# Weights stationary, tokens moving: turning the first product of two feed-forwards round, from the third chunk on

## The chip, the core and the metric

The kernel runs on one core of a Trainium2 chip, as one program in one launch. The engines named here are TensorE (matrix products and transposes, "PE"; its weight loads are a row of their own, "PEld"), VectorE ("DVE"), ScalarE ("ACT"), GpSimd ("POOL") and SyncE ("SP", which issues most DMAs). On-chip memory is SBUF for operands and PSUM for the results of TensorE. The metric is the device time of one execution in microseconds (us), and lower is better. Three runs of the kernel before gave a median of 793.23 us, from 792.94 to 793.36.

## The reference, cut to what matters

One layer of a residual block on 256 tokens of width 1024: a feed-forward, a mixer of two branches, a cross-attention on a memory, and a second feed-forward. Everything is in float32. Only the two feed-forwards are touched; both are this:

```
x = x + 0.5 * rmsnorm(swiglu(rmsnorm(x, pre_g), w_in, w_down), post_g)
def rmsnorm(x, g):  return x * rsqrt(mean(x*x) + 1e-6) * g
def swiglu(h, w_in, w_down):
    gate, up = split(h @ w_in, 2)          # w_in 1024 x 5632
    return (silu(gate) * up) @ w_down      # w_down 2816 x 1024
```

The per-token factor of the first rmsnorm can be taken out of the product: h @ w_in is that factor times (x * pre_g) @ w_in. So the kernel multiplies the unnormalised x and applies the factor, called r2 (one number per token, for each half of 128 tokens), to the results.

## The kernel before

**Split operands.** A float32 number is held as two parts, hi (rounded by a copy to the matmul type) and lo (what is left). A product of two such numbers is made of three: hi with hi, hi with lo, lo with hi, added up in PSUM. Each weight unit is 128 rows by 1024 columns (512 KB): `load_split` loads it as `raw` (4 buffers), ScalarE casts `hi` (line 142) and VectorE subtracts `lo` (line 144). `hi` and `lo` have 8 buffers each, used in turn; a new unit can be cast only when the unit eight places earlier is no longer read by TensorE. A unit of `w_in` holds two blocks of 128 contracted rows by 512 columns, so a chunk of the feed-forward has four units; a chunk of `w_down` has two.

**The feed-forward** (`ffn`, line 352) goes over 11 chunks of 256 hidden columns (`NFF` = 11). A chunk's first product gives 256 gate and 256 up columns, 512 in all. In the token form (`proj_tok`, line 184) the 128 tokens of one half are stationary and the 512 weight columns move: 8 contraction blocks by 3 products for each half, so 48 matmuls of 512 columns for a chunk. `act_evac` (line 370) takes a half's result out of PSUM: ScalarE applies silu to the gate with the scale r2, VectorE multiplies up by r2 and by that. The result has tokens on the partitions; the second product needs hidden columns there, so `flush` (line 358) makes four transposes on TensorE, and `split` (line 161) copies hi and subtracts lo from the transposed tile. `down` (line 401) is the second product of a chunk: 24 matmuls of 512 columns for both halves, into four PSUM banks that stay open over all chunks.

**Order.** After the first product of chunk c comes the second product of chunk c-2, with the transposes of chunk c placed 21 matmuls into it (`L_ACT`). Chunks 8 to 10 (`STAG` = 3) are left for a tail, first half of the tokens first, with `post` or, at the very end of the kernel, `post_last` for the second rmsnorm and the addition to x. In the first feed-forward chunks 0 to 2 are done in a form that goes over the contraction outermost, both halves at once (`act_first`), because the weights are still arriving. In the second, chunks 0 and 1 are done for one half of the tokens while the other half of x is not ready.

**Who orders the rest.** The program's order gives priorities; a planner places each engine's instructions by its own estimates, and `after(i)` ties instructions to the i-th matmul of a running log. Each engine then works in its own fixed order, so an instruction that waits holds all behind it on that engine.

**PSUM.** Eight banks: four `acc`, two `mm`, two `tr` (function `trp`).

**The row of factors.** Where tokens lie along the free dimension, a factor per token must be a row on all partitions. `row_of` (line 270) makes it for other stages: VectorE transposes a small tile that holds the factors (line 273), GpSimd's queue writes it to DRAM (line 275) and reads it back to all partitions (line 277).

`proj_col` (line 193) is a form used elsewhere in the kernel in which the weights stand and 256 tokens move, three matmuls of 256 columns per contraction block.

Of the kernel before, what the change touches and what calls it, by code (L numbers as in the profile page):

```python
# [36 lines left out]
L_LAST = 8  # L37
# [42 lines left out]
def block_kernel(ctx: ExitStack, tc: tile.TileContext, wts, head_in, gf_in, x_in, mem_in, memT_in, cols, rows, fbias, masks, out):  # L80
# [102 lines left out]

    def proj_tok(ps, X, units, h, n=512):
# [64 lines left out]
    def ssq(dst, src):  # L249
        S.activation(junk[:, : src.shape[-1]], src, AF.Square, accum_out=dst)  # L250
# [9 lines left out]
    fac = [cp.tile([P, 64], F32, name=nm("fac")) for _ in range(2)]  # L260
# [49 lines left out]
    def post(ps, h, grow, factor=1.0, store=False):  # L310

        s = s1(2, name="ss2")
        ts = []
        for j in range(2):
            ssq(s[:, j : j + 1], ps[j])
            t = sp.tile([P, 512], F32, tag="z2", name=nm("post"), bufs=3)
            V.scalar_tensor_tensor(out=t, in0=ps[j], scalar=-factor * SC_RSTD, in1=grow[:, j * 512 : (j + 1) * 512], op0=ALU.mult, op1=ALU.mult)
            ts.append(t)
# [6 lines left out]
    def post_last(ps, h, grow, factor):  # L325

        s = s1(2, name="ss2")
        ts = []
        for j in range(2):
            ssq(s[:, j : j + 1], ps[j])  # L330
# [9 lines left out]
            V.scalar_tensor_tensor(out=t, in0=ps[j], scalar=-factor * 16.0, in1=grow[:, j * 512 : (j + 1) * 512], op0=ALU.mult, op1=ALU.mult)  # L340
# [11 lines left out]
    def ffn(w_in, w_dn, X, r2, n_tok, i_row, first_half, second_half=None):  # L352

# [16 lines left out]
        def act_evac(ps, c, h):  # L370
            sg = sp.tile([P, FC], F32, tag="c1", name=nm("sg"), bufs=7)
            silu = S.activation(sg, ps[:, :FC], AF.Silu, scale=r2[h])  # L372
            if c == NFF - 1 and h == 1 and not first_half:
                with tc.issue_after(silu.ins):
                    S.activation(warm, ones[:, 0:1], AF.Abs_reciprocal_sqrt)
            a = sp.tile([P, FC], F32, tag="c1", name=nm("at"), bufs=7)
            V.scalar_tensor_tensor(out=a, in0=ps[:, FC:], scalar=r2[h], in1=sg, op0=ALU.mult, op1=ALU.mult)  # L377
# [4 lines left out]
        def act_tok(c, h):  # L382
            ps = mm()
            proj_tok(ps, X, chunk(w_in, c), h)
            act_evac(ps, c, h)

# [26 lines left out]
        for h in range(2):  # L413
# [3 lines left out]
            if h == 0 and n_tok:  # L417
                second_half(m)
        accs = None
        done = 0  # L420
        if callable(r2):
            outs = act_first((0, 1), acc)
            r2 = r2()
            for c in range(2):
# [4 lines left out]
        for c in range(n_tok, NFF):  # L429
# [7 lines left out]
            else:  # L437
                for h in range(2):
                    n = len(log)
                    act_tok(c, h)  # L440
                    if c == 2 or c > NFF - STAG + 1 and h == 0:
                        flush(n + L_ACT)
# [7 lines left out]
            while done < min(c - 1, NFF - STAG):  # L450
# [795 lines left out]
```

## Time and profile before

| what | value |
|---|---|
| median of 3 runs | 793.23 us (792.94 to 793.36) |
| profiled execution, its own time | 791.78 us |
| its span, first to last instruction | 790.0 us |
| clock granted to TensorE | 0.998 of full speed |
| PE busy / weight loads busy | 99% / 86% |
| VectorE / ScalarE / GpSimd busy | 66% / 54% / 2% |
| one chunk in the steady part of a feed-forward | 16.80 us |

Busy shares are over the whole span. In the chain that ended last, each piece is the work, or the wait, that the next one waited for, so its shares say where the time is. A TensorE row's mean duration is that of one matmul from its start to its modelled end; since matmuls overlap, what a matmul costs in a row of them is the distance between starts.

### The profile page before, as it was taken

To read this page: it belongs to the slowest core of one execution; us is meant where nothing else is said; L and a number is where in the kernel's file an instruction comes from. 1 tells how busy PE (TensorE), PEld (TensorE's weight loads), DVE (VectorE), ACT (ScalarE), POOL (GpSimd) and SP (SyncE) were. 2 spreads that over 40 slices of the span, in tenths; PEclk is the share of its full clock that TensorE was granted. 3 is DMA by queue.
4 is the path that set the end of the run, shared out by engine and by line. 5 is a ranking of instruction groups with operands and counts; after the bars stand their busy time and mean duration, and the time that the engine had idled before them with its cause. 6 is when DMAs were issued, how large, how long until landed. Compare 5 with 4: busy or idle time off the path is not lost.

```text
span 790.0 us, 12203 instructions
## 1 busy us (share of the span) xinstructions
PE 782.3 (99%) x4736; PEld 677.4 (86%) x4736; DVE 519.0 (66%) x825; ACT 426.8 (54%) x656; POOL 13.7 (2%) x36
## 2 busy tenths in 40 slices
PE   9999999999999999999999999999999999999996
PEld 7888888888899999998788888999888888888885
DVE  6774545557767899488686666964669754545543
ACT  7654444546664677357774345643657644434541
POOL 0000000000000102100000000000000000000000
PEclk9999999999999999999999999999999999999999
DMA  9786654563654547634576654555263655554521
GB/s 347 247 271 205 228 189 160 188 202 118 210 196 144 180 136 224 258 120 152 197 251 222 211 191 160 164 186 181 65 229 134 227 199 209 203 200 161 183 84 54
DMA packets 44345, 147.82 MB, mean 187 GB/s; under 512 B 5048, under 2 KB 8768, under 8 KB 44288
## 3 DMA queue, kind: packets, MB, share of 16 engines
q1 hardware_dynamic: 43168, 144.83, 53.9%
q0 software_dynamic: 688, 1.85, 1.0%
q8 instruction: 37, 0.61, 0.3%
q10 hardware_dynamic: 432, 0.37, 0.1%
q14 instruction: 20, 0.16, 0.1%
HBM read 145.97 MB, written 1.06 MB: 186 GB/s over the span
## 4 chain that ended last, share of the span: by engine, by line
PE 98%; DMA 1%; DVE 0%; ACT 0%; SPq 0%; issue 0%; DVEq 0%; ACTq 0%
PE mm L94 68%; PE acc L94 27%; PE tr L367 1%; PE tr L94 1%; PE tr L294 1%; DMA head<-in_head_dram 1%; PE tr L898 0%; PE tr L989 0%; PE acc L1099 0%; DVE xs L348 0%; DVE post L340 0%; ACT hi L507 0%; SPq L491 0%; ACT hT L285 0%; SPq L486 0%
## 5 line engine op out<-in xcount | busy, mean ns | idle before, releaser
L144 DVE TENSOR_TENSOR lo<-raw,hi 128x1024 fp32r<-128x1024 f32 (+1 forms) x256 | 306.7, 1206 | 122.4 <-ACT hi L142 114.3
L142 ACT CAST hi<-raw 128x1024 fp32r<-128x1024 f32 (+1 forms) x256 | 262.4, 1038 | 149.3 <-PE mm L94 83.3
L94 PE MATMUL mm<-lo,hT 128*128 128x512 f32 (+1 forms) x592 | 226.9, 385 | 0.0
L94 PE MATMUL mm<-hi,hT 128*128 128x512 f32 (+1 forms) x592 | 226.8, 385 | 0.0
L94 PE MATMUL mm<-hi,lT 128*128 128x512 f32 (+1 forms) x592 | 226.5, 385 | 0.0
L94 PEld LDWEIGHTS mm<-hi,lT 128*128 128x128 f32 x592 | 111.2, 188 | 21.4 <-DVE lT L286 0.2
L94 PEld LDWEIGHTS mm<-hi,hT 128*128 128x128 f32 x592 | 111.2, 188 | 21.4 <-ACT hT L285 0.3
L94 PEld LDWEIGHTS mm<-lo,hT 128*128 128x128 f32 x592 | 111.0, 188 | 20.7
L94 PE MATMUL acc<-hi,act 128*128 128x512 f32 x352 | 111.8, 390 | 0.0
L94 PE MATMUL mm<-hT,lo 128*128 128x256 f32 x384 | 109.0, 284 | 0.0
L94 PE MATMUL mm<-hT,hi 128*128 128x256 f32 x384 | 108.9, 284 | 0.0
L94 PE MATMUL mm<-lT,hi 128*128 128x256 f32 x384 | 108.8, 283 | 0.0
L94 PEld LDWEIGHTS acc<-hi,act 128*128 128x128 f32 x352 | 66.0, 188 | 13.6 <-DVE act L163 0.4
L94 PEld LDWEIGHTS mm<-hT,hi 128*128 128x128 f32 x384 | 73.6, 192 | 0.1
L94 PEld LDWEIGHTS mm<-lT,hi 128*128 128x128 f32 x384 | 73.6, 192 | 0.1
L94 PEld LDWEIGHTS mm<-hT,lo 128*128 128x128 f32 x384 | 73.6, 192 | 0.1
L94 PE MATMUL acc<-lo,act 128*128 128x512 f32 x176 | 69.7, 398 | 0.0
L372 ACT ACTIVATE sg<-mm,rstd 128x256 f32<-128x256 f32 x40 | 19.0, 475 | 75.8 <-PE mm L94 75.8
L377 DVE SCALAR_TENSOR_TENSOR at<-mm,rstd,sg 128x256 f32<-128x256 f32 x40 | 19.2, 481 | 57.4 <-ACT sg L372 57.4
L94 PEld LDWEIGHTS acc<-lo,act 128*128 128x128 f32 x176 | 33.1, 188 | 6.1
L94 PE MATMUL acc<-hi,hT 128*128 128x512 f32 x96 | 35.0, 392 | 0.5 <-ACT hi L507 0.4
L94 PE MATMUL acc<-hi,lT 128*128 128x512 f32 x96 | 35.1, 393 | 0.0
(198 smaller groups left out, 655.7 us busy)
## 6 DMA issues: line engine op xcount, KB each, us to landing
raw<-in_wts_dram SPq DMA_DIRECT2D x247, 512.0 KB, 4.4
raw<-in_gf_dram SPq DMA_DIRECT2D x12, 344.0 KB, 3.8
head<-in_head_dram SPq DMA_DIRECT2D x7, 392.0 KB, 6.6
grow<-in_rows_dram SPq DMA_DIRECT2D x4, 512.0 KB, 6.1
xs<-in_x_dram SPq DMA_DIRECT2D x2, 512.0 KB, 7.8
cbm<-cd POOLq DMA_DIRECT2D x2, 512.0 KB, 9.0
brow<-in_rows_dram SPq DMA_DIRECT2D x4, 256.0 KB, 4.6
memT<-in_memT_dram SPq DMA_DIRECT2D x2, 512.0 KB, 5.4
```

The costliest lines, as they stand in the source:

```text
L94: log.append(PE.matmul(*args, **kw).ins)
L142: S.copy(h, r)
L144: V.tensor_tensor(out=l, in0=r, in1=h.bitcast(F32), op=ALU.subtract)
L294: PE.transpose(ps[:, j * P : (j + 1) * P], src(kb), ident)
L367: PE.transpose(trv[:, j, h * P : (h + 1) * P], ats[c, h][:, j * P : (j + 1) * P], ident)
L372: silu = S.activation(sg, ps[:, :FC], AF.Silu, scale=r2[h])
L377: V.scalar_tensor_tensor(out=a, in0=ps[:, FC:], scalar=r2[h], in1=sg, op0=ALU.mult, op1=ALU.mult)
```

## The change

In the chunks from 3 on of the first feed-forward, and from 2 on of the second, the first product is done with the weights standing. Four blocks of 128 columns (two gate, two up) each get a PSUM bank. For each block `proj_both` first makes eight products of 512 columns: the hi part of the weights stands, and the hi and lo parts of 256 tokens, which the new class `Joined` keeps side by side, move in one product. Then come eight products of 256 columns: the lo part of the weights stands, the hi part of the tokens moves, and the result adds to the bank's first half. `added` copies the second half out with ScalarE and adds the first with VectorE. The result has hidden columns on the partitions already, so these chunks need no transposes.

The gate is multiplied by a row of r2, made by `row_of` twice more; up is not multiplied, and the factor that is missing is applied per token in `post` and `post_last` (their `pre`). `act_evac` of the chunks in the old form drops its factor in the same way. The second product keeps its form; its chunk 7 now comes after the first product of chunk 10, so that no second product stands between the first products of chunks 9 and 10.

```
    def proj_both(ps, X, units, cb):
        a, b = cb * P, cb * P + P
        for part in range(2):
            for kb in range(KB):
                w = blk(units, kb)[part][:, a:b]
                if part:
                    MM(ps[:, :T], w, X.hi(kb), start=False, stop=(kb == KB - 1))
                else:
                    MM(ps, w, X.both(kb), start=(kb == 0), stop=False)

    def added(out, ps):
        two = len(out.shape) == 3
        lo = sp.tile([P, T], F32, tag="c1", name=nm("plo"), bufs=7)
        S.copy(lo, ps[:, T:])
        a, b = (t.rearrange("p (b t) -> p b t", b=2) if two else t for t in (ps[:, :T], lo))
        V.tensor_tensor(out=out, in0=a, in1=b, op=ALU.add)
...
+        def act_col(c):
+            u = chunk(w_in, c)
+            gate, up = (sp.tile([P, 2, T], F32, tag="z2", name=nm(n), bufs=3) for n in ("gate", "up"))
+            for j in range(2):
+                ps = mm()
+                proj_both(ps, X, u, j)
+                added(gate[:, j], ps)
+            V.tensor_tensor(out=gate, in0=gate, in1=bc(row, [P, 2, T], 1), op=ALU.mult)
+            silu = S.activation(gate, gate, AF.Silu)
...
+            for j in range(2):
+                ps = trp() if c > 2 else acc()
+                proj_both(ps, X, u, 2 + j)
+                added(up[:, j], ps)
+            V.tensor_tensor(out=up, in0=up, in1=gate, op=ALU.mult)
+            split(acts[c][:, 0], acts[c][:, 1], up)
...
             else:
-                for h in range(2):
-                    n = len(log)
-                    act_tok(c, h)
-                    if c == 2 or c > NFF - STAG + 1 and h == 0:
-                        flush(n + L_ACT)
+                n = len(log)
+                act_col(c)
+                flush(n + L_ACT)
+                flush(n + L_ACT + 20)
...
-            while done < min(c - 1, NFF - STAG):
+            while done < (NFF - STAG if c == NFF - 1 else min(c - 1, NFF - STAG - 1)):
...
-                if c == NFF - 1 and cut == left:
-                    flush(m + L_LAST)
                 down(c, 0, (cut,))
-        post(accs[0], 0, grow, 0.5, not first_half)
+        post(accs[0], 0, grow, 0.5, not first_half, r2[0])
...
-            post_last(accs[1], 1, grow, 0.5)
+            post_last(accs[1], 1, grow, 0.5, r2[1])
...
-    def ssq(dst, src):
-        S.activation(junk[:, : src.shape[-1]], src, AF.Square, accum_out=dst)
+    def ssq(dst, src, scale=1.0):
+        S.activation(junk[:, : src.shape[-1]], src, AF.Square, scale=scale, accum_out=dst)
...
     def post_last(ps, h, grow, factor, pre):
+        f, sc = times(pre, -factor * 16.0)
...
-            V.scalar_tensor_tensor(out=t, in0=ps[j], scalar=-factor * 16.0, in1=grow[:, j * 512 : (j + 1) * 512], op0=ALU.mult, op1=ALU.mult)
+            V.scalar_tensor_tensor(out=t, in0=ps[j], scalar=f, in1=grow[:, j * 512 : (j + 1) * 512], op0=ALU.mult, op1=ALU.mult)
```

`times` makes the per-token factor of that line with one small VectorE operation; without `pre` it leaves the old constants.

68 lines of the change are left out of this document (50 added, 18 removed).

## The prediction

> **What bounds the kernel now.** I read the page first (span, busy times, the shares of the chain that ended last), then that chain in order of time, then the timeline of TensorE where another stage already moves 256 columns, then busy times over single chunks, and last the groups of instructions for prices.
>
> ```profile
> span 790.0 us, 12203 instructions
> PE 782.3 (99%) x4736; PEld 677.4 (86%) x4736; DVE 519.0 (66%) x825; ACT 426.8 (54%) x656; POOL 13.7 (2%) x36
> PE 98%; DMA 1%; DVE 0%; ACT 0%; SPq 0%; issue 0%; DVEq 0%; ACTq 0%
> ```
>
> TensorE is the chain for 98% of the span: a change is worth what it takes from, or adds to, TensorE's own sequence, unless it makes TensorE wait. There is one weight load for each matmul (4736 of each). One chunk of the steady part, from the chain in order of time (start, us, what):
>
> ```profile
> 78.64 10.90 PE mm L94 x48
> 89.55 4.99 PE acc L94 x22
> 94.54 0.44 PE tr L367 x4
> 94.98 0.47 PE acc L94 x2
> 95.44 10.92 PE mm L94 x48
> ```
>
> ```profile
> L367 PE MATMUL tr<-ident,at 128*128 128x128 f32 x88 | 13.2, 272 | 0.0
> ```
>
> First product 10.91 us for 48 matmuls of 512 columns (227.3 ns each), second product 4.99 + 0.47 = 5.46 us for 24, four transposes 0.44 us; 16.80 us from one chunk to the next, nothing between; the last row, a group over the whole kernel, counts the transposes. The price of a 256-column matmul comes from the timeline of the stage at lines 580 to 594, where weights stand (first two and last of 117 rows):
>
> ```profile
> 221.75 0.28 PE L94 MATMUL mm<-hT,hi 128*128 128x256 f32 x1
> 221.87 0.28 PE L94 MATMUL mm<-lT,hi 128*128 128x256 f32 x1
> ...
> 235.67 0.28 PE L94 MATMUL mm<-hT,lo 128*128 128x256 f32 x1
> ```
>
> ```profile
> L94 PEld LDWEIGHTS mm<-hT,hi 128*128 128x128 f32 x384 | 73.6, 192 | 0.1
> ```
>
> (235.67 - 221.75) / 116 = 120.0 ns from start to start. Two of them cost 240.0 ns, one of 512 columns 227.3: each instruction has about 13 ns that does not scale with columns. A load lasts 192 ns by the last row, a group, and still the starts lie 120 apart: the loads lie beside the products, and what they cost is inside both prices.
>
> **The change, term by term.** Count of chunks: 8 in the first feed-forward (3 to 10), 9 in the second (2 to 10), 17.
>
> *Products.* A chunk loses 48 matmuls of 512 columns (10.91 us) and gets 4 blocks of 8 wide and 8 narrow: 32 x 227.3 = 7.27 us and 32 x 120.0 = 3.84 us, 11.11 us. Columns moved are equal; the 16 more instructions cost +0.20 us.
>
> *Transposes.* Four a chunk go, on the chain as quoted: -0.44 us. 68 of the 88 go; chunks 0 to 2 of the first and 0, 1 of the second keep theirs.
>
> *Sum.* -0.234 us a chunk, x 17 = -4.0 us.
>
> *The end.* The last `post_last` takes its factor per token and not as a constant. Its last steps are on the chain:
>
> ```profile
> 783.67 0.60 ACT L250 ACTIVATE junk<-acc 128x512 f32<-128x512 f32 x1 [3.39 <-PE acc L94]
> 784.39 0.69 DVE L340 SCALAR_TENSOR_TENSOR post<-acc,grow 128x512 f32<-128x512 f32 x1 [3.33 <-ACT junk L250]
> L544 ACT ACTIVATE iv<-mm,fac 128x512 f32<-128x512 f32 x4 | 2.7, 686 | 0.7 <-PE mm L94 0.7
> L844 DVE SCALAR_TENSOR_TENSOR G<-acc,rstd,G 128x512 f32<-128x512 f32 x4 | 2.8, 748 | 0.2
> ```
>
> The nearest rows with a factor per token are 0.686 and 0.748 us, against 0.60 and 0.69: +0.09 and +0.06, so +0.15 us; between 0 and that. I take all of it. The small operation that makes the factor needs only r2 and can be done long before.
>
> Against the profiled execution: span 790.0 - 4.0 + 0.15 = 786.1; that execution took 791.78, 1.78 around its span, so 787.9. The median of the runs is 1.45 above it: **789.4 us**.
>
> **Why I cost the rest at nothing.** *VectorE and ScalarE.* Busy time over a chunk of the first and one of the second feed-forward (the columns are PE, PEld, DVE, ACT, POOL, then clock and DMA), and groups:
>
> ```profile
> 78.64:95.44 16.80, 16.80 (x78) 13.91 (x77) 8.85 (x10) 7.65 (x10) 0.00 (x0) 1.00 0.62 217
> 739.00:755.80 16.80, 16.80 (x77) 13.90 (x77) 8.82 (x10) 7.63 (x10) 0.00 (x0) 1.00 0.57 189
> L142 ACT CAST hi<-raw 128x1024 fp32r<-128x1024 f32 x244 | 253.4, 1052 | 144.2 <-PE mm L94 78.3 <-PE acc L94 49.4 <-DMA raw<-in_wts_dram 13.2
> L144 DVE TENSOR_TENSOR lo<-raw,hi 128x1024 fp32r<-128x1024 f32 x244 | 296.4, 1223 | 117.6 <-ACT hi L142 109.7
> L163 DVE TENSOR_TENSOR act<-tr,act 128x512 fp32r<-128x512 f32 x22 | 15.1, 686 | 3.6 <-ACT act L162 3.6
> L162 ACT CAST act<-tr 128x512 fp32r<-128x512 f32 x22 | 12.9, 587 | 9.3 <-PE tr L367 9.3
> L802 DVE SCALAR_TENSOR_TENSOR k_b<-mm,row 128x256 f32<-128x256 f32 x8 | 3.0, 415 | 1.9 <-PE mm L94 1.9
> L372 ACT ACTIVATE sg<-mm,rstd 128x256 f32<-128x256 f32 x40 | 19.0, 475 | 75.8 <-PE mm L94 75.8
> L377 DVE SCALAR_TENSOR_TENSOR at<-mm,rstd,sg 128x256 f32<-128x256 f32 x40 | 19.2, 481 | 57.4 <-ACT sg L372 57.4
> L582 ACT ACTIVATE f<-f 128x512 f32<-128x512 f32 x4 | 2.5, 632 | 1.2 <-DVE f L581 1.2
> raw<-in_wts_dram SPq DMA_DIRECT2D x247, 512.0 KB, 4.4
> ```
>
> VectorE gets 4 adds of 256 columns (0.415 to 0.481 each; 0.42, the row that also reads one tile of PSUM and one of SBUF), two multiplications of 512 and the same subtraction as before (0.69 each): 3.75 us for the 2 x 0.48 + 0.69 = 1.65 it had. That is 8.85 + 2.1 = 10.95 us of a chunk of 16.57, 66%. ScalarE gets 4 copies of 256 columns (0.475 at most), a silu (0.63) and a copy of 512 (0.59): 3.1 for 1.54, 9.2 us, 56%. Room is left on both, so the question is one of lateness.
>
> A PSUM bank is not wanted back for 8 us or more: gates use the two `mm` banks, ups the two `tr`, and the next chunk's gate comes after two more blocks (5.56 us) and a second product (5.46).
>
> Weights are the tighter case. The third and fourth unit of the next chunk wait for the places of this chunk's first two, as the cast's releaser "PE mm L94" in the group above shows. Before, the first place came free at 5.46 + 1.36 = 6.8 us into the chunk. Now the lo part of unit one is read until the narrow pass of the last block: 8.33 + 1.82 + 0.24 = 10.4 us. From there VectorE has, in the worst order, four subtractions (4.9) and the last block's add, multiplication and subtraction (1.8): done at 17.1. The next narrow pass wants the third unit at 16.57 + 1.82 + 0.48 = 18.9. 1.8 us are left, which is why I count no wait; the hi parts, free at 8.8 and wanted at 17.5, have more. The second product's two units have a further 11 us. Raw loads (4 buffers) go out later by the same 3.6 us, but the load's own time is 4.4 us and the DMA engines are 62% busy in that stretch.
>
> Between chunks 9 and 10 no second product lies as cover. There the late units of chunk 10 take the places of the second product of chunk 6, free 11.1 us before chunk 10 begins. In the tail chunk 10's result is wanted 24 + 12 matmuls after its last block, 8.2 us, for some 3 us of work; the leftover chunk 7 is that cover, and without it the time would be 2.7 us.
>
> *The row of factors.* Rows from timelines, the chain and the line of the last DMA (factors of the first feed-forward, its chunk 3; factors of the second; a row as it is made now; chunks 0 and 1 of the second):
>
> ```profile
> 22.88 0.15 DVE L246 TENSOR_SCALAR rstd<-y 128x1 f32<-128x1 f32 x1
> 45.04 10.90 PE mm L94 x48
> 610.83 0.14 DVE L246 TENSOR_SCALAR rstd<-y 128x1 f32<-128x1 f32 x1
> 417.52 0.25 DVE L273 STREAM_TRANSPOSE runs<-fac 128x64 f32<-128x64 f32 x1
> 418.06 0.63 POOL L275 DMA_DIRECT2D rd<-runs  x1 [96.16 <-DVE runs L273]
> 423.57 0.56 POOL L277 DMA_DIRECT2D row<-rd  x1 [4.88 <-DMA rd<-runs]
> DMA to landing us min/median/max: 5.6/6.2/6.7
> 608.67 16.76 PE mm L94 x73
> ```
>
> From 417.52 to 423.57 + 6.7 = 430.3 is 12.8 us, the slower of the two rows made now. In the first feed-forward that gives 36 us, and the row is wanted 5.56 us into chunk 3, at 50.6. In the second it gives 611.0 + 12.8 = 623.8. Chunk 2 starts 48 matmuls after 608.67, at 619.6; its gates are both out of PSUM at 619.6 + 5.56 + 0.44 + 0.9 = 626.5. If the row came later, VectorE would stand at the gate's multiplication with the adds of up and the weights behind it. In this chunk up lies in two `acc` banks that the second product of chunk 0 wants back for the second half of the tokens, at 634.3. Three operations (1.5 us) come after the row, so TensorE waits only for a row later than about 633.
>
> **A rule against the change.** The quoted rows say 120.0 and 227.3 ns with a load in each. The Trainium skill, "TensorE: Matmul & The Clock Gate", "The mechanism" in Part 3, says that a weight load overlaps a running matmul only where the row groups differ, and "LDWEIGHTS (loading the stationary operand)" gives 1/1.2 ns a column, 106.7 for 128. Full-height loads would then stand in line, and an estimate by that rule is 17 x (16 x 0.107 - 0.44) = +21.6 us. The trace does not agree: 120.0 leaves no 106.7 beside the stream.
>
> **Rivals.**
>
> *Weights come late (slower).* If VectorE's order puts the second product's subtractions and the blocked evacuation ahead of the next chunk's third unit, 17.1 grows: the last block's copy can stand behind two casts (2.1 us) on ScalarE, and the add behind that holds the queue. A wait of w in each of 17 chunks decides from w = 0.234 us on; with w = 0.5 the time is 789.4 + 8.5 = 797.9. For it: one queue, later releases. Against: the orders in the trace follow what is wanted first, and 1.8 us of room remain in the worst order. 6%.
>
> *Narrow products cost more in this order (slower).* 120.0 was measured where two of three matmuls in a row use the same weights. Now every load is of new ones. The break-even is 127.3 ns; at 133 (the fixed 13 ns twice) a chunk costs 0.42 us more: 789.4 + 7.1 = 796.5. Against: every matmul has its own load anyway, and the starts are 0.12 apart row after row. 2%. If the loads are hidden only for weights that stand already, the 16 more loads stand in line at 0.192: 17 x 16 x 0.192 = 52 us more, 841. 1%; the rule above is of this kind.
>
> *Single waits eat part (about the same).* At the end of the first feed-forward stand these rows of the timeline and the chain:
>
> ```profile
> 186.23 1.41 DVE L321 SCALAR_TENSOR_TENSOR xs<-post,y,xs 128x512 f32<-128x512 f32 x2
> 187.94 0.87 PE tr L294 x8
> ```
>
> The transposes of x start 0.3 us after their x; with 0.15 more in `post`, and a changed order of the small operations, one subtraction (1.2 us) may come in between. The row of the second, or the banks of its chunk 2, may cost another 1: 791.5 to 792.5. 6%.
>
> *The fixed cost is mostly not paid (faster yet).* If the 13 ns came from the change of operands and not with each instruction, a narrow pass would cost half of a wide one, 113.7 ns: 17 x 0.20 = 3.5 us less, 785.9. Against: the 256-column rows. 3%. Of this kind is "Back-to-back issue gap" on the same page of the Trainium skill, N / 2.4 + 2.5 ns, 215.8 and 109.2 here; an estimate from it makes the extra instructions 0.04 us a chunk and the time 786.7. The rows of this trace are higher than both.
>
> **How the numbers follow.** Forecast 82%, in 788.4 to 790.6 (the sum, plus up to about 1 us of single waits). 0.2% of 793.23 is 1.6 us, about what a measurement of this kernel tells from no change; faster means under 791.6. Faster 0.86 (forecast, faster yet, and a little of the partial waits), same 0.05, slower 0.09. For 8 in 10 the range runs from 788.0 to 791.8, which adds the lower end of the partial waits and leaves out the slower cases and the fastest.
>
> **What would show it.** Chunks in the chain 16.57 us apart, with 11.11 for the first product and no "tr L367" after chunk 2; narrow rows 0.12 apart; 20 transposes left; TensorE's count up by 17 x (64 - 48 - 4) = 204 to 4940. It is wrong if the waits of TensorE name "lo" or "hi" of a weight or an "acc" bank, if narrow starts lie over 127 ns apart, or if VectorE's multiplication by the row waits for a DMA beyond 633 us.

## The result, and the profile after

The changed kernel takes 789.77 us (median of 14 executions, 789.44 to 791.66) against 792.11 us of the kernel before on the same chip (14 executions, 791.69 to 793.68). The ratio is 0.9971, 95% interval 0.9963 to 0.9979: faster by 2.3 us, and by 1.7 to 2.9 us over the interval. Forecast were 789.4 us, 3.8 below the 793.23 then known.

That the time came so near the forecast is partly luck. The median of three executions was 1.1 us above the median of 14, and the gain was forecast 1.5 us too large; the two errors nearly cancel. In the profiled executions the span went from 790.0 to 788.3 us (own times 791.78 and 790.07), 1.7 us, where 3.85 were forecast. So the question is where 2.2 us of the expected gain went.

The page of the changed kernel, with the span and the busy times:

```profile
span 788.3 us, 12740 instructions
...
PE 779.8 (99%) x4940; PEld 684.7 (87%) x4940; DVE 546.1 (69%) x899; ACT 441.2 (56%) x707; POOL 15.8 (2%) x42
```

The granted clock was 0.999 of full speed. TensorE has 4940 matmuls, 204 more than before, as counted. One chunk of the first feed-forward in the chain, in order of time (start, us, what; `mm` is the gate, `tr` is up, `acc` the second product):

```profile
78.57 5.56 PE mm L93 x32
84.12 5.59 PE tr L93 x32
89.71 5.47 PE acc L93 x24
```

The transposes are gone, nothing stands between the products, and the next chunk begins at 95.18, 16.61 us later (before: 16.80). The first product takes 5.56 + 5.59 = 11.15 us, not 11.11. VectorE and ScalarE over one chunk of each feed-forward (busy times of PE, PEld, DVE, ACT, POOL, then clock, DMA share and GB/s):

```profile
78.57:95.18 16.61, 16.61 (x89) 14.34 (x89) 10.40 (x15) 8.54 (x12) 0.00 (x0) 1.00 0.64 224
720.66:737.28 16.62, 16.62 (x90) 14.34 (x89) 10.50 (x15) 8.55 (x12) 0.00 (x0) 1.00 0.56 195
```

In the rows of the matmuls, all waits that the trace of the changed kernel names lie in the start, before the first chunk of the new form (us in total, times, longest us). The rows of the weight loads name a few short ones more, of which below.

```profile
PE tr L93 <- PEq L1296: 0.8, 1, 0.8
PE acc L93 <- ACT hi L568: 0.6, 1, 0.6
PE acc L93 <- ACT hlT L326: 0.2, 1, 0.2
```

**Where the 2.2 us went.** I cut both spans at the starts of the same matmuls. The starts are read from the trace, in us from the span's start:

| stretch | before | after | difference | due by the forecast |
|---|---|---|---|---|
| start to first matmul of the second product, chunk 0 | 38.96 | 39.22 | +0.26 | 0 |
| to the last matmul of the first feed-forward | 151.98 | 150.75 | -1.23 | -1.9 |
| to the first 256-column matmul of the stage behind it | 22.89 | 23.15 | +0.26 | 0 |
| to the second feed-forward | 383.38 | 383.35 | -0.03 | 0 |
| its chunks 0 and 1 | 23.07 | 23.29 | +0.22 | 0 |
| its chunk 2 to the second product of chunk 2 | 45.44 | 45.44 | 0.00 | -0.3 |
| to the last matmul of the kernel | 117.47 | 115.80 | -1.67 | -1.9 |
| to the span's end | 6.80 | 7.30 | +0.50 | +0.15 |

The last column is worked out with the forecast's prices: +0.20 for each first product and -0.44 for each set of four transposes in that stretch (8 and 8 in the first feed-forward; 3 and 2 up to the second product of chunk 2, since the transposes of chunk 4 stood inside that product; 6 and 7 behind it). The differences add up to -1.7.

**The first product.** The timeline of TensorE over the chunk that follows the one shown (a row is a group of matmuls that started one behind another; start and span):

```profile
95.02 1.98 PE L93 MATMUL mm<-hlT,hi 128*128 128x512 f32 x8
96.83 1.11 PE L93 MATMUL mm<-hlT,lo 128*128 128x256 f32 x8
97.78 2.00 PE L93 MATMUL mm<-hlT,hi 128*128 128x512 f32 x8
99.62 1.12 PE L93 MATMUL mm<-hlT,lo 128*128 128x256 f32 x8
```

The first eight wide matmuls, which come behind wide ones, take 96.83 - 95.02 = 1.81 us. The next eight, which come behind narrow ones, take 99.62 - 97.78 = 1.84. The single starts show how (ns from one start to the next, read from the trace; the first matmul behind transposes starts 80 early, so 313 stands for 233):

```
wide behind narrow     234 236 228 232 231 227 227 226
narrow behind wide     114 119 120 120 120 120 120 120
wide behind transposes 313 224 231 236 228 233 231 226     (kernel before)
```

Behind a change of width the first five wide matmuls come up to 9 ns late, about 27 ns together, and the first two narrow ones 7 ns early. So each return to wide costs about 0.02 us, and there are four in a chunk: three inside the first product, one at the start of the second. The kernel before paid the like once in a chunk, behind its transposes: about 0.03 us in the chunk of that row, 0.05 in the one ahead of it.

**The end of the first feed-forward.** The subtractions of weights among the small operations of the norm, from the timeline of VectorE in the kernel before and then in the changed kernel, there with the update of x:

```profile
184.90 1.23 DVE L144 TENSOR_TENSOR lo<-raw,hi 128x1024 fp32r<-128x1024 f32 x1
```

```profile
183.55 1.22 DVE L143 TENSOR_TENSOR lo<-raw,hi 128x1024 fp32r<-128x1024 f32 x1
184.96 1.23 DVE L143 TENSOR_TENSOR lo<-raw,hi 128x1024 fp32r<-128x1024 f32 x1
186.10 1.41 DVE L363 SCALAR_TENSOR_TENSOR xs<-post,y,xs 128x512 f32<-128x512 f32 x2
```

The chain there:

```profile
186.86 0.09 issue
186.94 0.63 PE tr L335 x4
187.57 0.24 PE acc L93
187.81 0.47 PE tr L335 x4
```

Between the first small operation of the norm and the update of x stood one subtraction of a weight before, and now there are two: 3.56 us (182.54 to 186.10) in place of 2.54 (183.69 to 186.23). TensorE's transposes of x, 0.87 us in one piece before, now come in two pieces of 0.63 + 0.47 with 0.09 of waiting ahead of them: 0.32 us more.

**The end of the kernel.** The last part of the chain, the changed kernel first and then the kernel before:

```profile
781.40 0.02 issue
...
782.29 0.75 DVE post L383
...
784.28 0.79 DVE xs L391 x2
```

```profile
783.59 0.02 issue
...
784.39 0.69 DVE post L340
...
786.32 0.79 DVE xs L348 x2
```

From the end of the last products to the end of the last x are 3.67 us now (785.07 - 781.40) and 3.52 before (787.11 - 783.59): +0.15, the forecast's term to the digit. But the span then ends 788.3 - 785.07 = 3.2 us later, and 790.0 - 787.11 = 2.9 before. In the trace of the changed kernel the closing part on GpSimd takes about 0.36 us longer, and so it does in all kernels built on it. What makes it longer is not shown.

### The profile page after: what moved, and what is told of

It is laid out like the page before. It is cut to its first block, busy times and chain, and to the rows that moved or that the text cites. A ratio compares the mean times of both kernels' runs of the same rounds, so it can differ in the third digit from the quotient of the medians.

```text
span 788.3 us, 12740 instructions
## 1 busy us (share of the span) xinstructions
PE 779.8 (99%) x4940; PEld 684.7 (87%) x4940; DVE 546.1 (69%) x899; ACT 441.2 (56%) x707; POOL 15.8 (2%) x42
## 4 chain that ended last, share of the span: by engine, by line
PE 98%; DMA 1%; DVE 0%; ACT 0%; issue 0%; SPq 0%; DVEq 0%; ACTq 0%
PE mm L93 56%; PE acc L93 28%; PE tr L93 12%; PE tr L335 1%; DMA head<-in_head_dram 1%; PE tr L959 0%; PE tr L412 0%; PE tr L1050 0%; PE acc L1160 0%; DVE xs L391 0%; DVE post L383 0%; ACT hi L568 0%; ACT hlT L326 0%; SPq L552 0%; SPq L547 0%
## 5 line engine op out<-in xcount | busy, mean ns | idle before, releaser
L93 PE MATMUL mm<-hi,lT 128*128 128x512 f32 (+1 forms) x272 | 103.5, 381 | 0.0
L93 PE MATMUL mm<-hi,hT 128*128 128x512 f32 (+1 forms) x272 | 103.1, 380 | 0.0
L93 PE MATMUL mm<-lo,hT 128*128 128x512 f32 (+1 forms) x272 | 102.9, 379 | 0.0
L93 PE MATMUL mm<-hlT,hi 128*128 128x512 f32 x272 | 68.0, 391 | 0.0
L93 PE MATMUL tr<-hlT,hi 128*128 128x512 f32 x256 | 64.1, 392 | 0.0
L93 PEld LDWEIGHTS mm<-hi,lT 128*128 128x128 f32 x272 | 51.1, 188 | 8.7 <-DVE lT L327 0.3
L93 PEld LDWEIGHTS mm<-lo,hT 128*128 128x128 f32 x272 | 51.1, 188 | 8.4
L93 PEld LDWEIGHTS mm<-hi,hT 128*128 128x128 f32 x272 | 51.1, 188 | 8.4 <-ACT hT L326 0.2
L93 PEld LDWEIGHTS mm<-hlT,hi 128*128 128x128 f32 x272 | 49.7, 188 | 9.5
L93 PEld LDWEIGHTS tr<-hlT,hi 128*128 128x128 f32 x256 | 46.0, 189 | 8.2
```

What stands on the lines that cost most here:

```text
L93: log.append(PE.matmul(*args, **kw).ins)
```

## The experiments

Comparisons are with the kernel before on the same chip; the changed kernel's own ratio is 0.9971, and 0.001 is 0.8 us. The intervals are 0.6 to 1.2 us on either side, so a difference between two kernels by their times is known to about 1 us; the stretches of the traces are finer. Stretches are those of the table above, in the order there: the first feed-forward 150.75, chunk 2 of the second 45.44, its last part 115.80.

### Wide and narrow in turn

Is it the change of width that costs, or the number of instructions? Wide and narrow alternate in each contraction block, 64 changes a chunk in place of eight.

```
-        for part in range(2):
-            for kb in range(KB):
+        for kb in range(KB):
+            for part in range(2):
```

> Only the order in a block of 128 columns is changed: wide, narrow, wide, narrow, and not eight wide and then eight narrow. The sums are the same. In the changed kernel the first five wide starts after narrow ones lie 233, 236, 228, 233, 231 ns apart (227 later on), and the first narrow one 113 (120 later): a change from narrow to wide and back costs about +20 ns net, four times a chunk. Theory A, each change has its price: 32 changes a chunk in place of 4, 28 x 0.020 x 17 = +9.5 us over the changed kernel's 789.8, so about 799, slower than before. Theory B, the price is a ramp that only a long wide run pays: a pair of wide and narrow costs 233 + 113 = 346 against the 347 of steady starts, so the four ramps a chunk go, 0.08 x 17 = -1.4 us, about 788.4. Neither: within 0.5 us of 789.8.

Measured: 792.56 us, ratio 1.0010 (1.0002 to 1.0019), about 3 us over the changed kernel. The chain (start, us, what):

```profile
78.47 5.64 PE mm L93 x32
84.11 5.65 PE tr L93 x32
```

11.29 us for a first product in place of 11.15. A pair of one wide and one narrow goes in about 353 ns (233, 241, 236 for the wide and 117, 120, 113 for the narrow in turn), where 227 + 120 = 347 would be paid without changes. So a return to wide costs 6 to 7 ns when they come one by one, less than the 20 of a return to a long run of wide ones, but there are 32 in a chunk in place of four. Neither expectation was met: the cost is real, and it does not multiply by the number of changes.

### Four wide blocks, then four narrow

The other direction: one run of 32 wide and one of 32 narrow matmuls in a chunk, one return to wide in place of four.

```
+            banks = [mm(), mm()] + [trp() if c > 2 else acc() for _ in range(2)]
+            for j in range(4):
+                proj_both(banks[j], X, u, j, (0,))
             for j in range(2):
-                ps = mm()
-                proj_both(ps, X, u, j)
-                added(gate[:, j], ps)
+                proj_both(banks[j], X, u, j, (1,))
+                added(gate[:, j], banks[j])
...
+                proj_both(banks[2 + j], X, u, 2 + j, (1,))
```

> All four blocks of a chunk make their wide products first, into their four banks, then all four make their narrow ones: one change from narrow to wide in a chunk in place of four. Theory A and B alike: 3 x 0.020 x 17 = -1.0 us against the changed kernel, about 788.8, with a chunk period of 16.56 in place of 16.62. Rival, lateness: all four banks come out at the end of the chunk and the lo parts of the weights are held longer; if TensorE then waits for a bank, a weight or the second product's operand, each wait is named in TensorE's waits, and the time is 790 or more.

Measured: 790.87 us, ratio 0.9991 (0.9982 to 1.0000). The chain in a chunk (in the first feed-forward):

```profile
79.79 3.63 PE mm L93 x16
83.42 3.63 PE tr L93 x16
87.04 1.91 PE mm L93 x16
88.96 1.92 PE tr L93 x16
90.88 5.47 PE acc L93 x24
```

First product 11.09 us, period 16.55: three returns fewer save 0.07 us, 0.02 each, so the ramps are what the first product had over the forecast. The last part of the second feed-forward takes 115.44 us, 0.36 less than in the changed kernel. But the time is worse, and one place is the second feed-forward's chunk 2, which takes 46.51 us in place of 45.44. TensorE waits there, by the loads' waits and ScalarE's timeline:

```profile
PEld acc L93 <- ACT act L161: 1.1, 1, 1.1
```

```profile
637.95 0.62 ACT L161 CAST act<-up 128x512 fp32r<-128x512 f32 x1 [2.64 <-DVE up L446]
638.47 1.07 ACT L161 CAST act<-tr 128x512 fp32r<-128x512 f32 x2
```

TensorE wants the operand of chunk 0's second product (`act<-tr`, here still made by transposes, at 625.85). Its copy stands on ScalarE behind the copy of chunk 2's own result (`act<-up`), and that one waits 2.64 us for VectorE, because the evacuations of all four blocks now come at the very end, behind the narrow run, with subtractions of weights between them. This is a wait that the forecast's 8 us of spare time for the banks leaves out: the banks were free, and a copy was late in its engine's queue.

All these stretches together make about +0.5 us (-0.31 in the first feed-forward, +1.07 and -0.36 in the second, and some 0.07 between). The medians differ by more, 1.1 us; the profiled execution has 1.3 us more in the start, of which below, and whether this holds for the median is not shown.

### Three narrow products

The tokens' two parts do not move together: three products of 256 columns, as `proj_col` has them. ScalarE copies the result instead of `added`.

```
-                    MM(ps[:, :T], w, X.hi(kb), start=False, stop=(kb == KB - 1))
-                    MM(ps, w, X.both(kb), start=(kb == 0), stop=False)
+            MM(ps[:, :T], wh, X.hi(kb), start=(kb == 0), stop=False)
+            MM(ps[:, :T], wh, X.lo(kb), start=False, stop=False)
+            MM(ps[:, :T], wl, X.hi(kb), start=False, stop=(kb == KB - 1))
```

> Undoes one part of the change: hi and lo parts of the tokens no longer move in one product. A block is 24 products of 256 columns (the weights still stand), and the result is copied out by ScalarE alone, with no second half to add. By the price of an instruction that does not scale with columns (13 ns): 96 x 120.0 = 11.52 us a chunk for 11.15, less the ramps of three of the four changes (0.06): +0.31 to +0.37 x 17 = +5 to +6.3 us, 795 to 796. If the fixed price came from a change of the standing weights and not from the instruction, two of three products use the same weights and the time would be at or below 789.8.

Measured: 797.3 us, ratio 1.0067 (1.0055 to 1.0080), 7.5 us over the changed kernel and more than 5 over the one before.

```profile
79.23 5.75 PE mm L93 x48
84.98 5.76 PE tr L93 x48
```

11.51 us for 96 matmuls, 119.9 ns each, where two of three products use the same weights. In the changed kernel's narrow passes every load is of new ones, and the price is 120 as well: it comes with the instruction and not with the change of weights. The chunk costs 0.36 us more than in the changed kernel, 6.1 us over 17 chunks, and the spans of the two profiled executions differ by that (794.5 and 788.3); the medians differ by 1.3 more. The spans of the five executions are 794.5 and 794.6 in two and 795.5 to 796.2 in three, a difference of the size that the start alone can make, as told below; that it is this one is not shown. Without the joined move, turning the product round would have lost: a chunk then has 48 matmuls more than in the kernel before, 11.51 us in place of 10.91, and the four transposes are worth less than that.

### Transposes back

Four transposes of a constant come into 15 second products, where the kernel before had those of its chunks; nobody reads them, so this is extra work.

```
                 flush(n + L_ACT)
+                if c > 2 or not first_half:
+                    again = trp()
+                    with after(n + L_ACT):
+                        for i in range(4):
+                            PE.transpose(again[:, i * P : (i + 1) * P], ones, ident)
```

> Four transposes of a constant tile are put back into 15 second products of the changed kernel, where the transposes of the chunk stood before; nobody reads their result. If the transposes were worth what the chain showed for them (0.44 us a chunk, and some 0.03 for the ramp behind them), the time is 15 x 0.44 to 15 x 0.47 = +6.6 to +7.0 us: 796.4 to 796.8, slower than before. If their time was only partly TensorE's (hidden by weight loads or by idle time that others would fill), less than 5 us.

Measured: 797.22 us, ratio 1.0070 (1.0057 to 1.0083), 7.4 us over the changed kernel.

```profile
95.70 0.44 PE tr L522 x4
```

The period is 17.10 us, +0.48: the 0.44 of the transposes and 0.04 of the ramp behind them. 15 x 0.48 = 7.2, which is also the difference of the spans (795.5 and 788.3). So taking the transposes away is worth what it was said to be, in full; it is not given back by other engines.

### No chunk left over

Chunk 7's second product back in its place between the first products of chunks 9 and 10.

```
-            while done < (NFF - STAG if c == NFF - 1 else min(c - 1, NFF - STAG - 1)):
+            while done < min(c - 1, NFF - STAG):
```

> Undoes one part of the change: the second product of chunk 7 goes back between the first products of chunks 9 and 10, and after chunk 10's first product only 12 matmuls (2.7 us) lie before its own second product begins. In the changed kernel chunk 10's operand is ready 5.5 us after its last block (172.88 against 167.34), with the queue order that the cover allowed; the bare work is some 3 us. If the leftover is what covers this, TensorE waits 0.3 to 2.8 us at each of the two tails: +0.6 to +5.6 us, 790.4 to 795, and TensorE's waits name 'act'. If the planner fits it in, or if the leftover costs as much between chunks 9 and 10, the time stays within 0.5 us of 789.8.

Measured: 790.76 us, ratio 0.9987 (0.9978 to 0.9996), 1.3 us over the changed kernel by the ratios. In the trace the first feed-forward takes 151.01 us in place of 150.75 and the last part 116.07 in place of 115.80: 0.53 us in all. The matmuls' rows name no wait but in the start; the weight loads wait for the copy of the operand, `act`, 0.4 us at each of the two tails, as was expected if the leftover is what covers this. The profiled execution, the slowest of the 11, has a further 1.36 us in the start (first second-product matmul at 40.58 in place of 39.22), of which more below; so of the 1.3 us between the kernels 0.53 is shown, and the rest is open. By the forecast 2.7 us would be left in the tail for some 3 us of work, 0.3 us too little; the last part shows 0.27.

### Later transposes of x

The transposes of x at the end of the first feed-forward three matmuls later (24 to 27), to take away their wait.

```
-L_F1 = 24
+L_F1 = 27
```

> One number is changed: the transposes of the first half of x at the end of the first feed-forward come 3 matmuls later (0.68 us). In the changed kernel they start at 186.86, wait, are broken up by a matmul, and their second half of x is there only at 187.5; from chunk 10's end to the products that follow, 0.47 us more are spent than in the kernel before. If that is the single wait forecast there, 0.3 to 0.5 us come back: 789.3 to 789.5, and the eight transposes stand together again at 0.87 us in the chain. If the loss is elsewhere, no difference; if the products that follow then wait for the transposed x, up to 0.7 us worse.

Measured: 790.36 us, ratio 0.9979 (0.9971 to 0.9988): no gain. The chain of this kernel at that place:

```profile
187.17 0.97 PE tr L335 x8
```

The waits of the weight loads behind it:

```profile
PEld mm L93 <- DVE lT L327: 0.7, 2, 0.5
```

The transposes are in one piece again and the first feed-forward takes 150.53 us, 0.22 less. But the products that read the transposed x now wait for its lo parts (`lT`), and the stretch behind takes 23.52 us in place of 23.15. The wait moved by one stage.

### The same form in other stages

The f and q products of the mixer and the memory query products, three narrow passes, take the joined form as well.

```
-    X2 = Pair()
+    X2 = Joined()
...
-            ps = proj_col2(X2, u, (2 * j, 2 * j + 1))
-            V.tensor_tensor(out=fj, in0=halves(ps), in1=bc(row2h, [P, 2, 2, P], 1), op=ALU.mult)
+            for i in (2 * j, 2 * j + 1):
+                ps = mm()
+                proj_both(ps, X2, u, i)
+                added(f[:, :, i], ps)
+            V.tensor_tensor(out=fj, in0=fj, in1=bc(row2h, [P, 2, 2, P], 1), op=ALU.mult)
```

> The same turning for three other stages, where weights stand already and 3 products of 256 columns are made: the forget and query projections of the recurrence and the queries of the memory read get wide and narrow products and an added second half, with the bank per block that this needs. 192 pairs save 360 - 347 = 13.3 ns each, 2.6 us, less 24 changes from narrow to wide at 0.02, 0.5: about -2.1 us, 787.7, if the price per instruction is what the ledger says and the additional copies and adds (24 each) are hidden. VectorE is 67% busy from 220 to 262 us, and gets 0.42 for each block of 2.8 us; if that makes TensorE wait, 789.8 or more, with its waits naming 'f', 'z' or a weight's 'lo'.

Measured: 792.67 us, ratio 1.0008 (0.9999 to 1.0017), about 2.9 us over the changed kernel. The two feed-forwards are unchanged (150.75, 45.44, 115.80); from the first to the second are 409.09 us in place of 406.50. TensorE waits there (us in total, times, longest us; the second row lies ahead of the f products, the last behind the memory query products):

```profile
PE mm L93 <- DVE f L215: 1.8, 2, 1.2
PE mm L93 <- DVE lo L143: 0.8, 1, 0.8
PE tr L93 <- ACT hT L1134: 0.9, 1, 0.9
```

The first row is the wait for a bank. These stages use the two `mm` banks alone, and a block lasts 2.8 us. A bank comes free after a copy on ScalarE and an add on VectorE, and VectorE's queue has weights to subtract ahead of the add (218.72 to 219.86, the add behind it). It happens twice, both times in the f products; the blocks of the q and the memory query products wait for no bank. The other two rows are a late subtraction of a weight and a late copy on ScalarE. The matmuls are cheaper and these four waits cost more.

### Four and four from the third chunk

The order of four wide and four narrow blocks, but not in chunk 2 of the second feed-forward, and the later transposes of x.

```
-            for j in range(4):
+            for j in range(4 if c > 2 else 0):
...
-                proj_both(banks[j], X, u, j, (1,))
+                proj_both(banks[j], X, u, j, (1,) if c > 2 else (0, 1))
...
-L_F1 = 24
+L_F1 = 27
```

> All four wide passes ahead of all four narrow ones as in e2, but not in chunk 2 of the second feed-forward, where e2 waited (1.1 us for the second product's operand), and the transposes of x 3 matmuls later as in e6. Chunk period 16.55 for 16.62 in 16 chunks: -1.1 us; the wait at the end of the first feed-forward -0.3 to -0.5: about 788.2 to 788.5. If e2's loss was not that one wait, 789.8 or more.

Measured: 789.45 us, ratio 0.9968 (0.9955 to 0.9980). The feed-forwards take 150.42, 45.32 and 115.64 us, 0.6 less than in the changed kernel, and the stretch behind the first takes 0.37 more, as with later transposes alone. The wait of 1.1 us in chunk 2 is gone.

### The same with the transposes of x where they were

```
-L_F1 = 27
+L_F1 = 24
```

> The order of four wide blocks and then four narrow ones from the third chunk of each feed-forward on, as in the run with that order and later transposes of x, but with the transposes of x at the end of the first feed-forward where the changed kernel has them (24). That run gained 0.33 us in the first feed-forward and lost 0.37 us in the products that follow it, and this one is to tell which part came from the order and which from the later transposes. If the order alone is worth two changes of width less in each chunk: period 16.55 against 16.62, 16 chunks, 1.1 us less than the changed kernel, ratio to the kernel before 0.9957. If what the order saves is met again by a wait at the end of the first feed-forward: no more than 0.5 us less, 0.9965 or above.

Measured: 789.41 us, ratio 0.9968 (0.9956 to 0.9981). The stretches are 150.30, 23.17, 45.32 and 115.44: 0.45, 0.12 and 0.36 less than in the changed kernel, and nothing lost behind. So the order alone brings 0.9 us in these stretches of the 1.1 that 16 chunks with 0.07 each give, and the later transposes brought nothing. (The run with both has 0.2 us less gain in its last part: a weight load waits there 0.3 us for a `lo`.) The times cannot tell it from the changed kernel (intervals of 1 us on either side). It has the lowest median of the kernels here, 0.4 us under the changed kernel's, which is not shown to be a difference.

### Two of the three other stages

The q products and the memory query products in the joined form, the f products in three narrow passes.

```
+            z = sp.tile([P, 2, 2, P], F32, tag="z2", name=nm("z2"), bufs=3)
+            for i in range(2):
+                ps = mm()
+                proj_both(ps, X2, u, 2 * j + i)
+                added(z[:, i], ps)
+            V.tensor_tensor(out=z, in0=z, in1=bc(row2h, [P, 2, 2, P], 1), op=ALU.mult)
```

> Of the three further stages that were turned, only the q products and the memory query products are (lines 655 to 664 and 1113 to 1124); the f products, which stand right behind the first feed-forward, stay in three narrow passes. If the loss of that run came from the f products alone (TensorE waited there 1.8 us for the add into f and 1.4 us for the copy that frees a bank), the other two stages give what the price says: 16 blocks of 8 contraction blocks, (3 x 120 - 347) x 8 less 20 ns for a change of width, 0.085 us each, 1.4 us less than the changed kernel, ratio 0.9953. If two banks of mm, emptied by two instructions in a row on two engines, are too few in every stage with products this short (2.8 us a block): no gain or a loss, 0.9970 or above.

Measured: 795.5 us, ratio 1.0045 (1.0032 to 1.0059): slower than with all three. This is in the range of the second theory, but not by its mechanism: no wait for a bank is named. (The 1.8 and 1.4 us of the expectation overlap, as rows of matmuls and of weight loads; TensorE lost 1.8 there.) The chain of this kernel, and the busy times over the stretch behind (the clock is the third figure from the end):

```profile
269.33 1.81 PE acc L93 x120
271.14 1.15 PE mm L93 x6
272.28 3.12 issue
```

```profile
275.41:279.00 3.59, 3.59 (x14) 3.59 (x14) 0.00 (x0) 0.00 (x0) 0.29 (x2) 0.55 0.02 6
```

TensorE stands for 3.1 us in a stage that the edit does not touch, behind a burst of some 190 short matmuls, and the trace names no releaser. Then it runs at about half its clock (by the trace's clock records, 0.5 from 275.80 to 279.22): the matmuls of 344 columns lie 287 ns apart and not 158, 1.5 us more. Together, by the distances between starts, 4.8 us, and the stretch up to the second feed-forward is 3.84 longer, so the two stages did save about 1 us of the 1.4 expected. A further wait, 0.8 us for a weight's `lo`, lies just behind the first feed-forward (+0.88 in that stretch), which the run with all three stages has too.

What stops TensorE at 272.28 was not tested: with all three stages turned the same burst passes without a stop. The traces' records of DMA packets have a likely cause. Queue 8, of the kind "instruction", loads 16 KB for about every 250 matmuls and weight loads that TensorE executes, so I take these for TensorE's own instructions. In this kernel such a load comes at 257.3 us and the next only at 272.9, inside the stop, landing at 273.8. In the changed kernel one comes at 266.4 and with all three stages at 268.1, ahead of the burst.

### Both together

The edits of the last two runs in one kernel: the four wide and four narrow order from the third chunk, and the two other stages.

> Both of the other two edits together. If both hold: 2.5 us less than the changed kernel, ratio 0.9939. If neither: 0.9965 to 0.998. They touch different stages, so the gains and losses of the two should add within 0.4 us; if they do not, the end of one stage and the start of the next share a wait.

Measured: 795.73 us, ratio 1.0048 (1.0034 to 1.0063). The stop behind the burst is there again (4.0 us), after the same number of matmuls and weight loads (3264), and again with no load of instructions between 256.6 and 272.9 us. So the gains could not be seen to add. The first feed-forward keeps the gain of the order (150.27 us), but the last part does not (115.85): in its chunk 10 a weight load waits 0.3 us for the add that frees a gate's bank, which neither run alone has.

## Why the prediction was right, and where it was not

**What bounds the kernel.** Right. TensorE is the chain, the added work of VectorE and ScalarE lies beside it (10.4 to 10.5 us a chunk where 10.95 was forecast, 8.5 where 9.2), and what the transposes cost came back in full, as the run with transposes back shows from the other side.

**Products.** Right in kind, too low in size. The two prices hold, 227 and 120 ns, the narrow one whether the weights are new each time (120 in the changed kernel) or in one of three (119.9 with three narrow products). The step that failed is 32 x 227.3 + 32 x 120.0: it takes prices from long rows of one width, and leaves out the return from narrow to wide. With the returns the first product is 11.15 and the period 16.62, against 11.11 and 16.57: 0.05 x 17 = 0.85 us of the 2.2 missing. The single starts and the order with one return (11.09) show that this is the reason.

**The fixed 13 ns.** The forecast put "mostly not paid" at 3% and the Trainium skill's 2.5 ns beside it ("TensorE: Matmul & The Clock Gate", "Back-to-back issue gap", 215.8 and 109.2 ns here). The traces do not agree with either: 227 and 120 in steady rows, before and after.

**The rule against.** The full-height loads are hidden: 684.7 us of loads lie beside 779.8 of matmuls, and the estimate of +21.6 us did not come.

**Transposes.** -0.44 a chunk was right, a little low: with the ramp behind them they are worth 0.48 each.

**Weights late.** No wait on a weight is named in the changed kernel in any chunk of the new form, so the 1.8 us of room in the worst order were enough. The one wait on a `hi` (0.6 us) lies in the start, as in the kernel before (0.4).

**The row of factors.** Right, though the forecast let chunk 2 start 48 matmuls after 608.67, at 619.6, and it was 51, at 620.3; nothing hung on it. In the second feed-forward the row was read back by an issue on GpSimd's queue well before its use by VectorE:

```profile
616.91 0.57 POOL L318 DMA_DIRECT2D row<-rd  x1 [2.82 <-DMA rd<-runs]
```

```profile
627.35 0.69 DVE L436 TENSOR_TENSOR gate<-gate,row 128x512 f32<-128x512 f32 x1
```

**Costed at nothing: single waits.** This is the second term that failed. The forecast allowed up to 1 us and took none. They came: 0.32 at the end of the first feed-forward, by the mechanism that the rival named (one subtraction of 1.2 us between the norm and x), 0.26 in the stretch behind it, 0.22 in chunks 0 and 1 of the second feed-forward, and about 0.15 in its chunk 2 (0.3 due by the forecast, 0.15 by the measured prices, 0.00 seen). 0.95 in all. The first is shown by its rows. The second and third are waits of weight loads, nearly all for parts of the transposed x (`hT`, `lT`, `hlT`), which the trace names in the stretch behind the first feed-forward and then in chunks 0 and 1 of the second:

```profile
PEld mm L93 <- DVE lT L327: 0.3, 1, 0.3
PEld mm L93 <- ACT hT L326: 0.2, 1, 0.2
```

```profile
PEld mm L93 <- DVE hlT L327: 0.6, 2, 0.3
PEld mm L93 <- DVE y L265: 0.3, 1, 0.3
PEld mm L93 <- ACT hlT L326: 0.2, 1, 0.2
```

The kernel before has none in the first stretch and three of 0.2 to 0.3 us in the second. By the distances between starts TensorE loses 0.07 to 0.18 us at each of the places in the changed kernel. In chunk 2 the first matmul of the second product starts at 636.93, some 0.15 late, behind ScalarE's copy of its operand (to 636.88): the same copy that cost 1.1 us in the run with four wide blocks and then four narrow.

**The end.** +0.15 was right. The closing part at the program's end, +0.36, was not foreseen, and its cause is open; neither was the start (+0.26, which differs by more than that from one execution to the next).

The sum: 0.85 + 0.95 + 0.36 + 0.26 = 2.4 us, for 2.2 missing in the span; the 0.2 over is of the size of what prices rounded to 0.01 us make over 17 chunks. The gain by medians, 2.3 us, is larger than by the two spans, 1.7, because the profiled execution of before lay 0.3 below its median and that of after 0.3 above.

**The leftover chunk.** The 2.7 us that would be left for some 3 us of work were sized right: without it each feed-forward's end costs about 0.27 us, and the wait is for the operand.

## What to carry to other kernels

When a product is turned round to save transposes, price it by instructions and not by columns: a matmul here cost about 13 ns beside its columns, so joining two narrow moves into a wide one decided between a gain of 2 us and a loss of 5. Group matmuls of one width into long runs, but look first at what stands behind the later evacuation in the queues of the other engines: in one chunk that was another operand's copy, and it cost 1.1 us, more than the order gave in all other chunks (0.7). And do not carry the form to a stage because it paid in another: where two banks and blocks of 2.8 us were all there was, two waits for a bank, 1.8 us together, took most of what was to be gained (2.1).

## What the runs showed that I had not expected

**A ramp behind narrow matmuls.** 234, 236, 228, 232, 231 ns before the steady 227, and 114, 119 before the steady 120. Taken in turn, wide and narrow cost 353 ns a pair and not 347.

**The start is not the same in every execution.** The first matmuls of the first product, by TensorE's timeline, in the changed kernel:

```profile
4.67 1.20 PE L93 MATMUL acc<-hi,hlT 128*128 128x512 f32 x4 [0.56 <-ACT hi L568]
```

and in the run with four and four and the transposes of x where they were:

```profile
4.62 2.08 PE L93 MATMUL acc<-hi,hlT 128*128 128x512 f32 x4 [0.50 <-ACT hi L569]
```

Both start at the same time to 0.05 us, but the first four matmuls span 2.08 us in the second and 1.20 in the first. Read from the trace, the distances in the second are 594 ns, then eight of 427, one of 366, and from there 233; in the first most lie near 230. The first second-product matmul then comes at 40.32 us and not at 39.22. Over the traces here it lies at 38.96 to 39.31 in eight executions and at 40.1 to 40.6 in five. The traces' clock records go with it: full clock begins at 3.9 to 6.9 us in the eight (4.46 in the changed kernel) and at 8.3 to 9.6 in the five (8.91 in the other). Each kernel has one trace, but no edit here touches the products of the start, and the spans of the changed kernel's 14 executions run from 787.6 to 789.6 us. So up to 1.7 us between two single executions need not come from the edit, and the stretches above leave the start out. The Trainium skill, "TensorE: Matmul & The Clock Gate", "What's actually happening" in Part 1, has TensorE at half its clock until it has been busy for about 3.4 us, by a window that does not start with the kernel. The traces agree: the slow distances end where the record of full clock begins, and 427 is 1.88 times the steady 227.

**Half the clock behind a stop of 3.1 us.** The run with two other stages shows it: behind the stop TensorE runs at half clock for 3.41 us, and loses 1.5 us beside the stop itself. The run with both together has the same 3.41 us behind a stop of 4.0, so the half-clock stretch did not grow with the stop. The same section says that TensorE falls back to half its clock after an idle window of about 3.4 us. The traces agree roughly: here a stop of 3.1 us was long enough.
